# A hybrid retention/HGRN2 trunk on one core: where the HGRN2 state and row transfers are requested, and when the sample updates run

## The chip, the core and the metric

The kernel runs on one core of one Trainium2 chip. The metric is the device time of one execution in microseconds (us), taken as the median of several runs. One further execution was recorded by the hardware profiler; every row shown below comes from that execution, and its clock starts at the first instruction of the program.

## The reference, cut to what matters

One step of a decoder layer is computed for 272 prompt tokens (16 learned ones ahead of 256) and 8 sample tokens that go on from a stored state. Both groups use the same weights. The layer is a half-step feed-forward block, a mixer and a second half-step feed-forward block, each behind a residual and a layer norm.

```python
x <- LN1(alpha*x + 0.5*SwiGLU_1(x))
x <- LN2(alpha*x + Mixer(x))
x <- LN3(alpha*x + 0.5*SwiGLU_2(x))

# Mixer: x @ w_in, 2048 -> 10*2048, cut into
# [q_ret | k_ret | v_ret | g_ret | q_hg | f_hg | i_hg | g_hg | gate_ret | gate_hg]
def hgrn2_chunk(S, q, k, v, logf):
    b = jnp.cumsum(logf.astype(jnp.float32), axis=2)
    ...
    A = jnp.einsum('bhid,bhjd,bhijd->bhij', q, k, decay)
    o = jnp.einsum('bhij,bhjv->bhiv', A, v) + jnp.einsum('bhid,bhdv->bhiv', q * jnp.exp(b).astype(q.dtype), S)
    ...
    S_new = jnp.exp(b_last[:, :, 0, :, None]) * S + jnp.einsum('bhjd,bhjv->bhdv', k_dec, v)
```

The change lies in the HGRN2 half of the mixer. It has 16 heads with a 128x128 state each. For a sample token the chunk has one position, so its new state is `f * S + k v^T`, with `f` and `k` one number per state row and `v` one row of 128 numbers; its output is `q` times the new state. Eight samples make eight such states per head, 512 KB, which come from memory, are updated and go back.

## The kernel before, in words

**The weight stream.** Nearly all of the time is TensorE multiplying a stream of weight blocks of 128x128. `stream` fetches them eight at a time: a 512 KB transfer into a buffer `raw` (L185, issued on SyncE's queue), a cast to a rounded high part `whi` on ScalarE (L188) and the rest `wlo` on VectorE (L189). `dense` (L218) then makes three matmuls per block: high by high, high by low, low by high. `raw`, `whi` and `wlo` have three buffers each. A transfer into `raw` therefore waits for the `wlo` three fetches earlier, and a cast waits for TensorE to be done with the buffer three fetches earlier. Eight blocks are 24 matmuls.

**The mixer.** The projection with `w_in` runs over eight units `u`, each with two HGRN2 heads and one retention head. For each unit `project` runs the groups f, q_h, i_h, q_r, k_r, v_r, each two output tiles over 16 values of `k`, and then the gate groups of the unit before. In the trace the accumulators of these groups are named `pj_f`, `pj_q_h` and so on.

**Threads and steps.** The mixing itself is written as generators, `mix_hg(u, ...)` and `mix_ret(u, ...)`, that are interleaved with the projection. After each `k` of a group `dense` calls `pump`, which counts every thread down by one and resumes those that are due. `yield n` in a generator means: go on `n` steps later. A step of a two-tile group is six matmuls of the weight stream. TensorE runs in exactly the order in which the code issues its instructions. The order on the other engines, and on SyncE's queue of transfers, is made by a scheduler out of that same program; each engine and the queue then work strictly in order.

**The HGRN2 thread.** It scales q and k by levels, makes the score group and goes on as follows.

- The score group, `blocks` (L817 to L827) and `upper` (L843 to L853): 80 small products with an output `pl` in PSUM, issued without a weight matmul between them. Products in plain float32 take two matmul instructions each, and every matmul instruction has a weight load of its own.
- `fill` (L829, for head 0 and then head 1): VectorE moves part of `pl` into the score tile `acc` (`acch` in the trace), by masks, six instructions each plus one multiplication. `keep` (L857) moves the rest on ScalarE.
- `turned(h)` (L966): transposes of K and a ScalarE copy into `kts[h]` (`kth`).
- `gate()` (L975): the factors f and k of the sample tokens as columns of `meta`.
- `samples(h)` (L984): for each of eight samples, a scaling of the state `smh` on ScalarE (L988) and the addition of the outer product on VectorE (L989), which reads the rows `vbh`; then the store `out_sgs`.
- The prompt states `Ss` (`pst` in PSUM), the sample outputs `pq`, and the prompt outputs.

**The four transfers per unit.** `load(h)` (L765) asks for the states of head `h` (`smh`, 512 KB, L771) and `values(h)` (L773) for the eight rows of `v`, spread over all partitions (`vbh`, 512 KB, L776). `smh` shares its two buffers with two operands of the score group (`Qm`), `vbh` with another (`kept`).

**A tie.** `load(1)` and `values(1)` first let GpSimd copy one column of a result into the target buffer (L770 from `acc`, L775 from `kts`). The transfer writes over that column, so it can't be issued before the copy, and the copy can't run before the result is there. The queue is in order, so a transfer that waits for its tie also holds up what stands behind it.

Units 0 and 1 have other waiting times than the steady units 2 to 7 (`steady = u > 1`).

Of the kernel before, what the change touches and what calls it, by code (L numbers as in the profile page):

```python
# [18 lines left out]
P = 128  # L19
# [109 lines left out]
def trunk(ctx: ExitStack, tc: tile.TileContext, A, O):  # L129
    nc = tc.nc  # L130
# [12 lines left out]
    def mx_bank(name):  # L143
        return ps_m.tile([P, 512], F32, tag="mx", name=name)
# [59 lines left out]
    def dense(block, nk, outs, xhi, xlo, cols=slice(0, T), hook=None, parts_in_turn=False):  # L204
        n = len(outs)
        if isinstance(cols, slice):
            cols = [cols] * n
        for k in range(nk):
            todo = []
            for i in range(n):  # L210
                wh, wl = block()
                h, l = xhi[k][cols[i]], xlo[k][cols[i]]
                o = pairs(outs[i][:, : 2 * h.shape[1]])
                todo.append([(o, wh, h, k == 0, False), (o, wh, l, False, False), (o, wl, h, False, k == nk - 1)])

            for x in zip(*todo) if parts_in_turn else todo:
                for o, w, t, start, stop in x:
                    nc.tensor.matmul(o, w, t, start=start, stop=stop)  # L218
            if hook is not None:
                hook(k)  # L220
# [59 lines left out]
    class Norm:  # L280
# [96 lines left out]
        def first(self, block, outs, x0s):  # L377


            n = self.n  # L380

            def hook(k):
                if k == 5:
                    self.stats()

            dense(block, KC, outs, xh, xl, [slice(x0, n + 2) for x0 in x0s], hook)
            ys = self.corrected(outs, x0s)
            for c in range(KC):
                d = self.d[c]
                sub(d, d, self.mean)  # L390
                nc.vector.scalar_tensor_tensor(
                    out=d, in0=d, scalar=self.g[:, c : c + 1], in1=self.r, op0=ALU.mult, op1=ALU.mult)
            return ys

        def second(self, block, outs, x0s, into=()):
            dense(block, KC, outs, xh, xl, [slice(x0, self.n + 2) for x0 in x0s])
            self.normalise()
            return self.corrected(outs, x0s, into)
# [148 lines left out]
    with tc.tile_pool(name="yp", bufs=1) as yp:  # L547
# [7 lines left out]
        with tc.tile_pool(name="mp", bufs=1) as mp:  # L555
# [7 lines left out]
            def tmp(name, shape=(P, T), bufs=1, dt=F32, tag=None):  # L563
                if name in rows:
                    rows[name] = rows[name][1:] + rows[name][:1]
                    return rp.tile(list(shape), dt, tag=rows[name][-1], name=name)
                return mp.tile(list(shape), dt, tag=tag or name, name=name, bufs=bufs)
# [80 lines left out]
            def evacuate(n, c0, c1, o0, o1, b0, b1):  # L648
# [14 lines left out]
                elif n == "i_h":  # L663
                    v = st.pop("i_h", None)
                    if v is None:
                        v = tmp("v", (P, 2, T))
                        nc.scalar.copy(v[:, 0, :], o0)
                        nc.scalar.copy(v[:, 1, :], o1)

                    start(mix_hg(c0 // 2, st["f"], st["k"], st["q"], v), {0: 20, 2: 46}.get(c0, 4))  # L670
                elif n in ("q_r", "k_r"):
                    sc, w, x0 = (1.0, TL, NMETA) if n == "q_r" else (KSC, T, 0)
# [73 lines left out]
            def mix_hg(u, f, k, q, v):  # L746
# [15 lines left out]
                acc = tmp("acch", (P, 2 * SEQ))  # L762
                sms, vbs = [], []

                def load(h):  # L765

                    sms.append(tmp("smh", (P, NS, P), bufs=2))
                    vbs.append(tmp("vbh", (P, NS, P), bufs=2))
                    if h:
                        nc.gpsimd.tensor_copy(sms[h][:, 0, :1], acc[:, 31:32])  # L770
                    nc.sync.dma_start(sms[h], A["sg"][2 * u + h])  # L771

                def values(h):  # L773
                    if h:
                        nc.gpsimd.tensor_copy(vbs[h][:, 0, :1], kts[h][:, 0, :1])  # L775
                    nc.sync.dma_start(vbs[h], vrow[h].partition_broadcast(P))  # L776


# [21 lines left out]
                def join(s):  # L800
                    _, m, t2 = sides(s)
                    Ts[2 * s] = tmp(f"T{2 * s}", (P, 2, m))
                    mul(Ts[2 * s], t2[:, :, :, 0], t2[:, :, :, 1])
# [25 lines left out]
                def fill(half, s, h):  # L829
                    a = acc[:, 2 * P * h : 2 * P * (h + 1)]  # L830
                    if s == 1:
                        nc.vector.tensor_tensor(
                            out=a.rearrange("p (b j c) -> p b j c", b=2, j=4),
                            in0=half[:, :, 48:].unsqueeze(2).to_broadcast([P, 2, 4, 32]),
                            in1=ident.rearrange("p (j c) -> p j c", j=4).unsqueeze(1).to_broadcast([P, 2, 4, 32]), op=ALU.mult)
                    for i, (sl, mi) in enumerate(((s, MASKS[s][0]), (2 * s, MASKS[2 * s][0]), (2 * s, MASKS[2 * s][1]))):
                        n = 16 // sl
                        nc.vector.copy_predicated(
                            a.rearrange("p (b j n t s) -> p b j n t s", b=2, j=4, t=2, s=sl)[:, :, :, :, 1, :],
                            msk[:, mi, :P].rearrange("p (b j n s) -> p b j n s", b=2, j=4, s=sl),  # L840
                            half[:, :, 16 * i : 16 * i + 16].rearrange("p b (n s) -> p b n s", s=sl).unsqueeze(2).to_broadcast([P, 2, 4, n, sl]))
# [104 lines left out]
                scale_k(64)  # L946
                scale_q(64)
                join(64)
                load(0)
                values(0)  # L950
                for h in range(2):
                    if u:
                        fill(first(h), 1, h)
                    fill(second(h), 4, h)
                    yield 4
                    if h == 0:
                        load(1)
                for s in (16, 32, 64):
                    keep(tops[s], s)
                yield 15 if u == 1 else 2  # L960
# [3 lines left out]
                kts = []  # L964

                def turned(h):  # L966
                    kt = tmp("kth", (P, 2, P), bufs=2)
                    kts.append(kt)
                    pt = mx_bank("ptk")
                    for b in range(2):  # L970
                        t0 = NMETA + b * P
                        nc.tensor.transpose(pt[:, b * P : (b + 1) * P], K[:, h, t0 : t0 + P], ident)
                    nc.scalar.copy(kt, pt[:, : 2 * P].rearrange("p (b f) -> p b f", b=2))

                def gate():  # L975
                    pt = mx_bank("ptm")
                    x = pt[:64, :P]
                    nc.tensor.transpose(x, meta.rearrange("p h t -> p (h t)"), ident)
                    for i in range(2):
                        nc.gpsimd.tensor_copy(meta[:, :, NMETA + NS * i : NMETA + NS * (i + 1)], fk[:, i])  # L980
                    for i in range(2):
                        upper_upper_lower(km[:, i, :], x[32 * i : 32 * i + NMETA], 32 * i)

                def samples(h):  # L984
                    vb, sm = vbs[h], sms[h]
                    for b in range(NS):
                        at = NMETA + b
                        nc.scalar.activation(sm[:, b, :], sm[:, b, :], AF.Copy, scale=meta[:, h, at : at + 1])  # L988
                        nc.vector.scalar_tensor_tensor(  # L989
                            out=sm[:, b, :], in0=vb[:, b, :], scalar=meta[:, h, at + NS : at + NS + 1], in1=sm[:, b, :],  # L990
                            op0=ALU.mult, op1=ALU.add)
                    nc.sync.dma_start(O["sgs"][2 * u + h], sm)

                turned(0)
                yield 2
                turned(1)
                values(1)
                yield (11, 10, 5)[min(u, 2)]
                gate()
                samples(0)  # L1000
                yield (6, 6, 4)[min(u, 2)]
                samples(1)
                yield (4, 5, 6)[min(u, 2)]

                Ss = []
                for h in range(2):
# [9 lines left out]
                            out=S[:, b + 1, :], in0=S[:, b, :], scalar=Tt[:, h, b : b + 1],  # L1016
                            in1=pst[:, (b + 1) * P : (b + 2) * P], op0=ALU.mult, op1=ALU.add)
                    nc.sync.dma_start(O["sgp"][2 * u + h], S[:, 2, :])
                yield (8, 6, 52)[min(u, 2)]
                pq = mx_bank("pq")  # L1020
                for h in range(2):
                    for b in range(NS):
# [339 lines left out]
```

## Time and profile before

| what | value |
|---|---|
| median of three runs | 2591.33 us (2587.07 to 2593.44) |
| the profiled execution, its own time | 2588.29 us |
| its span, first to last instruction | 2586.5 us |
| TensorE busy | 2560.9 us, 99% |
| VectorE, ScalarE, GpSimd busy | 66%, 54%, 2% |
| transfers on SyncE's queue, share of 16 DMA engines | 63.3% |
| projection with `w_in`, eight units | about 770 to 1787 us |

The chain of waits is followed back from the last instruction; "issue" in it is time in which an engine waited for nothing that the profile names. In the timeline a row is one instruction, or several of one kind merged (xN); the number in square brackets is the idle time ahead of it and what ended it. A window's row gives for each engine the busy time and the number of instructions, then the granted TensorE clock, the share of the DMA engines' time and the rate in GB/s.

### The profile page before, as it was taken

The page shows a single profiled execution, that of the slowest core. Times are in us where ns is not written, and L with a number is a line of the kernel's source. Part 1 is how long each engine was busy: PE and PEld are TensorE (multiplying, and loading weights), DVE is VectorE, ACT ScalarE, POOL GpSimd, SP SyncE. Part 2 cuts the span into 40 slices and gives each one's busy share as a digit, 9 for nine tenths or more (in the row PEclk, how much of TensorE's full clock was granted, in tenths as well). Part 3 has the DMA queues.
Part 4 walks back from the last instruction along what each step waited for, and adds up shares of the span by engine and source line. Part 5 has one row for each costly group of instructions (what it writes and reads, how often), then busy time and mean ns, then how long its engine had stood idle before and what let it go on. Part 6 is the DMA issues. An engine that isn't in the chain of part 4 may idle for free.

```text
span 2586.5 us, 56251 instructions
## 1 busy us (share of the span) xinstructions
PE 2560.9 (99%) x23424; PEld 2541.4 (98%) x23424; DVE 1701.5 (66%) x2827; ACT 1392.2 (54%) x2186; POOL 50.4 (2%) x136
## 2 busy tenths in 40 slices
PE   9999999999999999999999999999999999999999
PEld 9999999999999999999999999999999999999998
DVE  6544445475579878777777777777985555556555
ACT  5444444444456767766666666665564444444444
POOL 0000000000000000000000000000000000000000
PEclk9999999999999999999999999999999999999999
DMA  7555555555566776767676767676566666656664
GB/s 242 186 182 187 185 183 187 182 186 182 185 199 196 273 272 224 252 204 255 202 259 212 259 199 262 211 240 196 191 190 198 194 195 196 196 195 195 196 196 148
DMA packets 156896, 536.26 MB, mean 207 GB/s; under 512 B 17952, under 2 KB 25952, under 8 KB 156640
## 3 DMA queue, kind: packets, MB, share of 16 engines
q1 hardware_dynamic: 156352, 532.37, 63.3%
q8 instruction: 183, 3.00, 0.5%
q14 instruction: 73, 0.60, 0.1%
q10 hardware_dynamic: 288, 0.29, 0.0%
HBM read 501.99 MB, written 30.61 MB: 206 GB/s over the span
## 4 chain that ended last, share of the span: by engine, by line
PE 93%; DVE 4%; issue 1%; DMA 1%; ACT 1%; POOL 0%; SPq 0%; ACTq 0%; DVEq 0%
PE up L218 36%; PE dn L218 18%; PE pj_q_r L218 3%; PE pj_g_r L218 3%; PE pj_a_r L218 3%; PE pj_k_r L218 3%; PE wo L218 3%; PE pj_g_h L218 3%; PE pj_a_h L218 3%; PE pj_v_r L218 3%; PE pj_i_h L218 3%; PE pj_q_h L218 3%; PE pj_f L218 3%; DVE wlo L189 1%; DVE xl L421 0%
## 5 line engine op out<-in xcount | busy, mean ns | idle before, releaser
L189 DVE TENSOR_TENSOR wlo<-raw,whi 128x1024 fp32r<-128x1024 f32 (+1 forms) x869 | 1063.2, 1224 | 763.6 <-ACT whi L188 760.5
L188 ACT CAST whi<-raw 128x1024 fp32r<-128x1024 f32 (+1 forms) x870 | 905.4, 1042 | 924.0 <-PE up L218 410.9
L218 PE MATMUL up<-xh,wlo 128*128 128x280 f32 (+1 forms) x2624 | 725.8, 280 | 0.4 <-DVE wlo L189 0.3
L218 PE MATMUL up<-xh,whi 128*128 128x280 f32 (+1 forms) x2624 | 726.2, 280 | 0.0
L218 PE MATMUL up<-xl,whi 128*128 128x280 f32 (+1 forms) x2624 | 725.5, 279 | 0.0
L218 PEld LDWEIGHTS up<-xh,wlo 128*128 128x128 f32 x2624 | 492.6, 189 | 1.0 <-DVE wlo L189 1.0
L218 PEld LDWEIGHTS up<-xh,whi 128*128 128x128 f32 x2624 | 493.0, 189 | 0.1
L218 PEld LDWEIGHTS up<-xl,whi 128*128 128x128 f32 x2624 | 492.8, 189 | 0.0
L218 PE MATMUL dn<-hh,whi 128*128 128x280 f32 (+1 forms) x1376 | 384.7, 280 | 0.0
L218 PE MATMUL dn<-hl,whi 128*128 128x280 f32 (+1 forms) x1376 | 384.3, 279 | 0.0
L218 PE MATMUL dn<-hh,wlo 128*128 128x280 f32 (+1 forms) x1376 | 384.3, 279 | 0.0
L218 PEld LDWEIGHTS dn<-hh,whi 128*128 128x128 f32 x1376 | 260.1, 189 | 0.1
L218 PEld LDWEIGHTS dn<-hl,whi 128*128 128x128 f32 x1376 | 260.1, 189 | 0.1
L218 PEld LDWEIGHTS dn<-hh,wlo 128*128 128x128 f32 x1376 | 260.1, 189 | 0.0
L218 PE MATMUL pj_k_r<-xh,whi 128*128 128x280 f32 x256 | 75.1, 293 | 0.0
L218 PE MATMUL pj_g_r<-xh,whi 128*128 128x264 f32 x256 | 74.0, 289 | 0.0
L218 PE MATMUL pj_k_r<-xl,whi 128*128 128x280 f32 x256 | 73.3, 286 | 0.0
L218 PE MATMUL pj_v_r<-xh,whi 128*128 128x280 f32 x256 | 73.3, 286 | 0.0
L218 PE MATMUL pj_k_r<-xh,wlo 128*128 128x280 f32 x256 | 73.2, 286 | 0.0
L218 PE MATMUL pj_v_r<-xh,wlo 128*128 128x280 f32 x256 | 72.4, 283 | 0.3 <-DVE wlo L189 0.3
L218 PE MATMUL pj_g_h<-xh,whi 128*128 128x264 f32 x256 | 72.7, 284 | 0.0
L218 PE MATMUL pj_v_r<-xl,whi 128*128 128x280 f32 x256 | 72.3, 283 | 0.0
(419 smaller groups left out, 5276.9 us busy)
## 6 DMA issues: line engine op xcount, KB each, us to landing
raw<-in_w_up SPq DMA_DIRECT2D x343, 512.0 KB, 3.5
raw<-in_w_in SPq DMA_DIRECT2D x320, 512.0 KB, 4.2
raw<-in_w_dn SPq DMA_DIRECT2D x172, 512.0 KB, 3.4
smr<-in_sr SPq DMA_DIRECT2D x32, 512.0 KB, 5.1
out_srs<-smr SPq DMA_DIRECT2D x32, 512.0 KB, 6.9
raw<-in_w_out SPq DMA_DIRECT2D x32, 512.0 KB, 3.6
vbr<-vrd SPq DMA_DIRECT2D x32, 256.0 KB, 4.1
smh<-in_sg SPq DMA_DIRECT2D x16, 512.0 KB, 5.7
```

Of the source, the lines that this page charges most:

```text
L188: nc.scalar.copy(hi[:, j:jn, :], raw[:, j:jn, :])
L189: nc.vector.tensor_tensor(out=lo[:, j0:j1, :], in0=raw[:, j0:j1, :], in1=hi[:, j0:j1, :].bitcast(F32), op=ALU.subtract)
L218: nc.tensor.matmul(o, w, t, start=start, stop=stop)
```

## The change

Three things are changed, all in `mix_hg`.

1. All four transfers of a unit are now tied, and all stand behind the score group. The states of head 0 are requested behind the first `fill` and tied to `acc` of head 0. The rows of head 0 are requested behind the second `fill` and tied to `acc` of head 1. The states of head 1 are requested with `turned(0)` and tied to `kts[0]`. The rows of head 1 keep their place behind `turned(1)` and their tie to `kts[1]`.
2. In the steady units `turned(1)` comes 2 steps later and the sample updates 6 steps later than before (2 + 5 becomes 4 + 9). In units 0 and 1 the sum stays as it was (2 + 11 and 2 + 10 against 4 + 9, one step more in unit 1).
3. The prompt states come 5 steps later in the steady units, and the wait ahead of `pq` is shortened by 5, so that `pq` stands where it stood.

```diff
                     vbs.append(tmp("vbh", (P, NS, P), bufs=2))
-                    if h:
-                        nc.gpsimd.tensor_copy(sms[h][:, 0, :1], acc[:, 31:32])
+                    nc.gpsimd.tensor_copy(sms[h][:, 0, :1], kts[0][:, 0, :1] if h else acc[:, 31:32])
                     nc.sync.dma_start(sms[h], A["sg"][2 * u + h])
 
                 def values(h):
-                    if h:
-                        nc.gpsimd.tensor_copy(vbs[h][:, 0, :1], kts[h][:, 0, :1])
+                    nc.gpsimd.tensor_copy(vbs[h][:, 0, :1], kts[1][:, 0, :1] if h else acc[:, 2 * P + 31 : 2 * P + 32])
                     nc.sync.dma_start(vbs[h], vrow[h].partition_broadcast(P))
...
                 join(64)
-                load(0)
-                values(0)
-                for h in range(2):
+                for h, ask in enumerate((load, values)):
                     if u:
                         fill(first(h), 1, h)
                     fill(second(h), 4, h)
+                    ask(0)
                     yield 4
-                    if h == 0:
-                        load(1)
                 for s in (16, 32, 64):
                     keep(tops[s], s)
                 yield 15 if u == 1 else 2
...
                 turned(0)
-                yield 2
+                load(1)
+                yield 4
                 turned(1)
                 values(1)
-                yield (11, 10, 5)[min(u, 2)]
+                yield 9
                 gate()
                 samples(0)
                 yield (6, 6, 4)[min(u, 2)]
                 samples(1)
-                yield (4, 5, 6)[min(u, 2)]
+                yield (4, 5, 5)[min(u, 2)]
...
-                yield (8, 6, 52)[min(u, 2)]
+                yield (8, 6, 47)[min(u, 2)]
                 pq = mx_bank("pq")
```

What this makes of the transfers on SyncE's queue is the same in all steady units. Before, this stood there in unit 2 from the first row store on (`raw` with a number is a fetch of eight weight blocks, `vh0d` and `vh1d` the rows of `v` on their way through memory; TensorE comes to the score group of the unit at about the time at which `raw_12753` is issued):

```order
L730 DMA vh0d<-vsm 8x128
L185 DMA raw_12723<-in_w_in 128x1024
L730 DMA vh1d<-vsm 8x128
L776 DMA vbh<-vh0d 128x1024
L185 DMA raw_12753<-in_w_in 128x1024
L771 DMA smh<-in_sg 128x1024
L185 DMA raw_12821<-in_w_in 128x1024
L771 DMA smh<-in_sg 128x1024
L185 DMA raw_12868<-in_w_in 128x1024
L185 DMA raw_12916<-in_w_in 128x1024
L776 DMA vbh<-vh1d 128x1024
L185 DMA raw_12946<-in_w_in 128x1024
```

The same place of the queue now:

```order
L185 DMA raw_12759<-in_w_in 128x1024
L185 DMA raw_12800<-in_w_in 128x1024
L770 DMA smh<-in_sg 128x1024
L185 DMA raw_12857<-in_w_in 128x1024
L774 DMA vbh<-vh0d 128x1024
L185 DMA raw_12904<-in_w_in 128x1024
L770 DMA smh<-in_sg 128x1024
L185 DMA raw_12952<-in_w_in 128x1024
L774 DMA vbh<-vh1d 128x1024
L185 DMA raw_12987<-in_w_in 128x1024
```

`raw_12759` now is the fetch that was `raw_12753`. The rows of head 0 (`vbh<-vh0d`) moved back by three weight fetches, the states of head 0 by one, those of head 1 by two and the rows of head 1 by one; exactly one of the four stands between two fetches.

On ScalarE the sample updates stood here in unit 2 before, between the casts of the weights (`kth` is `kts`, `km` comes from `gate`, `v<-pj_v_r` is the first copy that the retention thread needs):

```order
L973 COPY kth<-ptk 128x256
L188 CAST whi_12869<-raw_12868 128x8x128
L723 CAST km<-ptm 16x128
L724 CAST km<-ptm 16x128
L988 ACTIVATE smh<-smh,meta 128x128 x5
L723 CAST km<-ptm 16x128
L724 CAST km<-ptm 16x128
L988 ACTIVATE smh<-smh,meta 128x128
L188 CAST whi_12917<-raw_12916 128x8x128
L988 ACTIVATE smh<-smh,meta 128x128 x7
L188 CAST whi_12947<-raw_12946 128x8x128
L988 ACTIVATE smh<-smh,meta 128x128 x3
```

And now, up to that copy:

```order
L723 CAST km<-ptm 16x128
L724 CAST km<-ptm 16x128
L983 ACTIVATE smh<-smh,meta 128x128 x2
L188 CAST whi_12953<-raw_12952 128x8x128
L723 CAST km<-ptm 16x128
L724 CAST km<-ptm 16x128
L983 ACTIVATE smh<-smh,meta 128x128 x6
L188 CAST whi_12988<-raw_12987 128x8x128
L983 ACTIVATE smh<-smh,meta 128x128 x7
L188 CAST whi_13054<-raw_13053 128x8x128
L983 ACTIVATE smh<-smh,meta 128x128
L1009 COPY Sh<-pst 128x128 x2
```

The sixteen scalings are the same sixteen; they now end two casts later, behind that of `raw_13053`. Before, the last of them stood behind the cast of `raw_12946`, with two more casts between them and the first `v` copy of the retention thread (L684); now that copy is the next row.

TensorE has the same matmuls; the transposes of `turned` and `gate` and the products `pst` stand 2, 6 and 5 steps later among the weight matmuls, and two waiting instructions are added in its program. GpSimd has sixteen more one-column copies in all.

## The prediction

> **What bounds the kernel now.** I read the page first, then TensorE's waits, then the chain of waits in order of time, and last the stretches that it pointed to. The page says that TensorE is the bound, and it gives the queue on which the program's own instructions are fetched (packets, MB, share of the DMA engines' time):
>
> ```profile
> span 2586.5 us, 56251 instructions
> PE 2560.9 (99%) x23424; PEld 2541.4 (98%) x23424; DVE 1701.5 (66%) x2827; ACT 1392.2 (54%) x2186; POOL 50.4 (2%) x136
> q8 instruction: 183, 3.00, 0.5%
> ```
>
> What TensorE waited for (us in total, times, longest) is one thing; every other cause of its waits adds up to 1.0 us or less:
>
> ```profile
> PE pj_q_r L218 <- issue: 15.1, 6, 3.1
> ```
>
> The chain shows where these six lie: each time a few matmuls behind the score group `pl` of a steady unit, in `pj_q_r` (start, length, what):
>
> ```profile
> 1003.27 1.12 PE pl L827 x89
> 1006.12 1.85 issue
> ...
> 1100.56 10.80 PE pj_q_h L218 x96
> ...
> 1131.45 1.07 PE pl L827 x89
> 1133.26 1.21 PE pj_q_r L218 x9
> 1134.47 3.13 issue
> ...
> 1263.85 1.07 PE pl L827 x89
> ...
> 1267.10 2.67 issue
> ...
> 1394.62 1.07 PE pl L827 x89
> ...
> 1398.10 2.32 issue
> ...
> 1523.23 1.07 PE pl L827 x89
> ...
> 1526.93 2.99 issue
> ...
> 1653.89 1.07 PE pl L827 x86
> ...
> 1657.81 2.18 issue
> ```
>
> The six sum to 15.14 us. There is more behind them. From one `pl` to the next it takes 128.18, 132.40, 130.77, 128.61 and 130.66 us; less the gap in each, 126.3, 129.3, 128.1, 126.3 and 127.7. So a unit without a gap is 126.3 us, and the gaps of 3.13, 2.67 and 2.99 are followed by a further loss of 3.0, 1.8 and 1.4 us. The windows show what it is (the third-last column is the granted clock, then the DMA share, then GB/s):
>
> ```profile
> 1003.27:1007.96 4.69, 2.85 (x167) 2.56 (x167) 4.14 (x8) 1.43 (x2) 0.00 (x0) 1.00 0.77 290
> 1131.45:1137.60 6.15, 3.02 (x170) 2.73 (x170) 5.07 (x16) 1.01 (x1) 0.00 (x0) 0.94 0.84 280
> 1137.60:1143.50 5.90, 5.90 (x26) 5.90 (x27) 1.52 (x4) 1.04 (x1) 0.19 (x1) 0.50 0.44 151
> 1394.62:1400.42 5.80, 3.48 (x175) 3.19 (x174) 4.72 (x14) 1.02 (x1) 0.00 (x0) 1.00 0.95 331
> 1523.23:1529.92 6.69, 3.70 (x175) 3.41 (x176) 5.30 (x16) 1.01 (x1) 0.19 (x1) 0.96 0.92 300
> ```
>
> After the gap of 3.13 us the clock is 0.50, and 26 matmuls take 5.9 us instead of 2.9 (the `pj_q_h` row gives 10.80/96 = 0.1125 us for one). After 2.32 us it stayed at full. The whole loss is 15.14 + 6.2 = 21.3 us; that is all the change can win here.
>
> **What I take the gap to be.** The q8 row has 183 packets; TensorE has 2 x 23424 instructions, so a packet brings 256.0 of them. The weight stream uses up 256 instructions (128 matmuls with their loads) in 128 x 0.1125 = 14.4 us. From `pl` at 1131.45 to the `pj_q_r` row at 1133.26, 1.8 us, pass the 160 matmuls of the score group (170 in the window's row, less 10 of the stream), 320 instructions. A border between two packets that falls early into the group thus needs the next packet within 2 to 3 us. The transfers just behind 1131.3 and just behind 1134.0, by queue:
>
> ```profile
> q1 hardware_dynamic: 186, 0.68, 80.1%
> ```
> ```profile
> q1 hardware_dynamic: 157, 0.57, 77.1%
> q8 instruction: 1, 0.02, 6.0%
> ```
>
> The first is 1131.3 to 1134.0, without a packet on q8; the second is 1134.0 to 1136.3, with one; TensorE stopped at 1134.47 and went on at 1137.60. So the instructions came late, at a time when the data queue kept the DMA engines 77 to 95% busy (the windows above). What stood on the queue:
>
> ```profile
> 1127.80 0.34 SPq L185 DMA_DIRECT2D raw<-in_w_in  x1
> 1128.18 0.32 SPq L730 DMA_DIRECT2D vh1d<-vsm  x1
> 1129.90 0.33 SPq L776 DMA_DIRECT2D vbh<-vh0d  x1
> 1131.05 0.33 SPq L185 DMA_DIRECT2D raw<-in_w_in  x1
> 1132.85 0.33 SPq L771 DMA_DIRECT2D smh<-in_sg  x1
> 1133.75 0.33 SPq L185 DMA_DIRECT2D raw<-in_w_in  x1
> 1137.96 0.33 SPq L771 DMA_DIRECT2D smh<-in_sg  x1
> ```
>
> **The change, part by part.** *The rows and states of head 0 leave the place ahead of the fetch.* `vbh` was requested 1.5 us ahead of the score group and is now three weight fetches later; `smh` was requested 1.4 us into the group and now waits for the first `fill`. The weight fetches of 1131.05 and 1133.75 stay, since they wait for buffers. The trace doesn't show the fetch without those two transfers, so I bound it. The busiest stretch of the projection gives the price of 512 KB:
>
> ```profile
> 840.00:845.00 5.00, 5.00 (x99) 4.78 (x98) 3.67 (x9) 4.99 (x6) 0.00 (x0) 1.00 1.01 404
> ```
>
> At 404 GB/s, 524 288 bytes keep all engines for 1.30 us. From below: nothing is saved, if the two weight fetches alone delay the packet as much. From above: both transfers were ahead of it, 2.60 us. I take 1.30 us per gap: `vbh` was ahead of the fetch in every unit, while `smh` was issued 1.1 us before 1134.0 and has moved little by then. The program also has two waiting instructions more on TensorE, both ahead of unit 2's score group; they shift the packet's border by one matmul against the group and take 0.11 us from the time allowed. The gaps become 0.66, 1.94, 1.48, 1.13, 1.80 and 0.99 us, together 8.0. All are below the 2.32 us that left the clock at full, so the 6.2 us go as well. Gain: 21.3 - 8.0 = 13.3 us. At the bounds: both saved leaves 0, 0.64, 0.18, 0, 0.50 and 0, so 20.0; none saved costs 0.7.
>
> [...]
>
> *Ties on the queue.* Four transfers per unit now wait for a GpSimd copy, and one weight fetch stands behind each. What such waits cost the queue before, beside what the weight fetches wait for anyway:
>
> ```profile
> SPq L185 <- DVE wlo L189: 1278.7, 580, 3.8
> ...
> SPq L771 <- POOL smh L770: 22.8, 6, 3.9
> ...
> SPq L776 <- POOL vbh L775: 13.3, 6, 2.7
> ```
>
> The weight fetches waited for a free buffer 580 times; two ties per unit held the queue for up to 3.9 us, and TensorE's waits show no weight that came late for it in the steady units. The new ties end before the buffer of the next weight fetch is free: head 0's two are results that stand ahead of the next `wlo` or just behind it on VectorE. I cost them at nothing; the cover is the three buffers, and a tie held longer than the 3.9 us seen is a price without a row. GpSimd's sixteen copies fall into its 98% of idle time.
>
> *Sample updates 6 steps later.* A step is six matmuls, 0.675 us, so 4.05 us. The same 16 scalings on ScalarE and 16 additions on VectorE run; what counts is whether they are done before the retention thread's `v` copy:
>
> ```profile
> 1164.11 1.05 ACT L188 CAST whi<-raw 128x1024 fp32r<-128x1024 f32 x1 [1.77 <-PE pj_v_r L218]
> 1166.73 0.39 ACT L684 COPY v<-pj_v_r 128x280 f32<-128x280 f32 x1 [1.57 <-PE pj_v_r L218]
> ...
> 1194.91 1.05 ACT L188 CAST whi<-raw 128x1024 fp32r<-128x1024 f32 x1 [2.26 <-DMA raw<-in_w_in]
> ```
>
> ScalarE stood idle for 1.77 + 1.57 = 3.34 us there, waiting for TensorE, and takes most of the 4.05; the remaining 0.7 us fall on weight buffers that are full. Cost: nothing, at most 0.7 us in six units.
>
> *Units 0 and 1.* Their sample updates stay, but head 0's rows move from an early request into the saturated stretches (404 GB/s above). At most 1.30 us each; I take nothing, since head 0's states leave the same stretches a little later too.
>
> *The sum.* 2588.29 (the profiled execution's own time) - 13.3 = 2575.0 us. That execution is 3.0 us below the median of the three runs; the mean of all four times is 2590.0, and 2590.0 - 13.3 = 2577 is what I forecast.
>
> **The rivals.** *The gaps close.* Both transfers were ahead of the fetch: gain 20.0, 2570 us. For it: the DMA share is 0.92 and 0.95 in the windows of 1523 and 1394. Against it: two weight fetches remain.
>
> *The gaps stay,* because the weight fetches alone delay the packet, or because something else makes them: 2590.0 + 0.7 = 2590.7 us. For it: in unit 2 the share was only 0.77 and there was a gap all the same. Against it: the gaps differ from 1.85 to 3.13 us at one and the same place of the program, so something outside TensorE sets their length.
>
> *The sample updates come too late,* the case that ends slower. Around 1194.91 ScalarE waits for weights that come just in time, so lateness that lasts until there would stop TensorE. If none of the idle time were usable, 4.05 us in six units are 24.3 us, against 13.3 won: 2601 us. It decides from 13.3/6 = 2.2 us of lateness per unit. Against it stands the 3.34 us of idle time ahead of the `v` copy.
>
> **How the numbers follow.** Forecast 0.50 (2573 to 2582); gaps close 0.18; gaps stay 0.20; samples late or weights held up 0.12. Forecast and closing are faster by more than 0.3% (7.8 us, about what a measurement can tell), 0.68; staying is within it, 0.20; lateness is slower, 0.12. The range goes from 2567, the closed gaps with 3 us of scatter between runs, to 2592, the gaps that stay; lateness is left out.
>
> **What the profile after would show.** Right: the "issue" waits of `pj_q_r` at the same place, six or fewer, about 8 us in total and none above 2.3; the clock full behind them; a unit 126 to 128 us from `pl` to `pl`. Wrong: "issue" still near 15 us, or new waits of TensorE for `wlo`, in `pj_v_r` or in the gate groups, which would mean late samples or held-up weights.

## The result and the profile after

The changed kernel takes 2576.74 us (median of 6 runs, 2575.6 to 2580.53) against 2587.7 us of the kernel before beside it (median of 6, 2582.48 to 2593.44): a ratio of 0.9958, 95% interval 0.9943 to 0.9972. It is faster by 11.0 us, or 0.42%. The forecast was 2577.

The page of the kernel after; its own time was 2577.58 us, against 2588.29 before:

```profile
span 2575.8 us, 56267 instructions
PE 2557.2 (99%) x23424; PEld 2536.8 (98%) x23424; DVE 1703.7 (66%) x2827; ACT 1391.9 (54%) x2186; POOL 52.7 (2%) x152
q8 instruction: 183, 3.00, 0.5%
```

The same 183 instruction packets and the same 23424 matmuls; only GpSimd has 16 instructions more, the new ties. What TensorE waited for (us in total, times, longest):

```profile
PE pj_q_r L218 <- issue: 7.8, 6, 1.7
...
PE po L1032 <- DVE Sh L1011: 0.6, 1, 0.6
...
PE pl L851 <- DVE Q L240: 0.3, 1, 0.3
```

The six gaps are still there, but half as long (15.1 before). The two other rows are new and small. The gaps stand at the same place as before, a few matmuls behind the score group (chain of waits, start, length, what):

```profile
1003.53 1.12 PE pl L825 x90
...
1006.78 0.52 issue
...
1130.89 1.07 PE pl L825 x89
...
1132.71 1.10 PE pj_q_r L218 x8
1133.81 1.70 issue
1135.51 3.62 PE pj_q_r L218 x16
...
1260.81 1.07 PE pl L825 x85
...
1263.94 1.62 issue
...
1388.87 1.07 PE pl L825 x89
...
1392.23 1.69 issue
...
1516.84 1.07 PE pl L825 x88
...
1520.43 1.25 issue
...
1644.37 1.07 PE pl L825 x89
...
1648.18 1.03 issue
```

The stretches from `pl` to `pl`, and the 3.42 us at half clock behind unit 3's gap of 1.70 us (length, busy time of PE, PEld, DVE, ACT and POOL, then granted clock, DMA share, GB/s):

```profile
1003.53:1130.89 127.36, 126.53 (x1278) 124.75 (x1282) 100.93 (x198) 86.65 (x162) 6.38 (x14) 1.00 0.71 240
1130.89:1260.81 129.92, 128.22 (x1280) 126.37 (x1283) 98.77 (x194) 84.75 (x158) 5.27 (x14) 0.99 0.70 232
1260.81:1388.87 128.06, 126.44 (x1279) 124.69 (x1283) 98.56 (x194) 84.87 (x158) 5.26 (x14) 1.00 0.71 236
1388.87:1516.84 127.97, 126.28 (x1280) 124.62 (x1283) 98.65 (x194) 84.73 (x158) 5.27 (x14) 1.00 0.70 236
1516.84:1644.37 127.53, 126.28 (x1279) 124.62 (x1283) 98.67 (x194) 84.59 (x158) 5.46 (x16) 1.00 0.70 237
...
1135.82:1139.24 3.42, 3.42 (x18) 3.42 (x17) 1.47 (x7) 0.24 (x1) 0.19 (x1) 0.50 0.30 65
```

TensorE's busy time is 126.3 to 126.5 us in four of the five stretches and 128.2 in unit 3: there 3.42 us ran at half clock behind a gap of only 1.70 us.

Where the time came from, by the two profiled executions (their spans differ by 10.7 us): up to unit 2 the kernel after is 0.26 us later (1003.53 against 1003.27). From unit 2's `pl` to unit 7's it takes 640.84 us in place of 650.62, a gain of 9.78. From there to the end 1.18 us are won, unit 7's gap being 1.15 us shorter (2.18 to 1.03). Of the 9.78 us, the five gaps give 6.18 (12.96 to 6.78) and the busy time of TensorE, which is nearly all the half clock, 3.91 (the five stretches of before had 126.33, 129.27, 128.10, 126.29 and 127.67); other small waits take 0.31 back.

The transfers by queue just ahead of and just behind 1133.1 us, in unit 3 of the kernel after:

```profile
q1 hardware_dynamic: 41, 0.14, 87.8%
```
```profile
q1 hardware_dynamic: 17, 0.06, 46.9%
q8 instruction: 1, 0.02, 21.4%
```

The first is 1132.7 to 1133.1, without a packet on q8; the second is 1133.1 to 1133.4, with one. TensorE went on at 1135.51. Before, the packet came after 1134.0, and it went on at 1137.60. On SyncE's queue only weight fetches are still requested close to the group; the four tied transfers follow behind them, with one fetch between each two (left out here):

```profile
1130.49 3.03 SPq L185 DMA_DIRECT2D raw<-in_w_in  x2
1137.43 0.33 SPq L770 DMA_DIRECT2D smh<-in_sg  x1
...
1141.78 0.36 SPq L774 DMA_DIRECT2D vbh<-vh0d  x1
...
1145.38 0.42 SPq L770 DMA_DIRECT2D smh<-in_sg  x1
...
1147.86 0.42 SPq L774 DMA_DIRECT2D vbh<-vh1d  x1
```

**The gap, counted.** Counted over TensorE's instructions in the trace (matmuls, weight loads and a few that only wait), the six gaps end at numbers 17857, 20417, 22977, 25537, 28097 and 30657. They are 2560 apart, ten packets of 256 exactly, while the score groups of neighbouring steady units begin 2556 or 2557 instructions apart. So the gap belongs to the border between two packets and not to a line of the program, and one border earlier lies inside the group: before, 79 to 98 instructions into its 320, after, 77 to 96. That earlier border is passed 0.4 to 0.5 us into the group. From there until TensorE goes on again took 4.4, 5.8, 5.6, 5.4, 6.3 and 5.7 us in units 2 to 7 before, and 3.5, 4.3, 4.4, 4.7, 4.5 and 4.5 us after. The difference is 1.2 us on the mean.

The trace also has the start of each instruction packet. It began 2.1, 2.3, 3.1, 3.2, 3.9 and 3.3 us behind that border before, and 1.1, 1.9, 2.2, 2.3, 2.3 and 2.2 us after. In all twelve cases TensorE went on 1.2 to 1.5 us after the end of the packet, so the length of the gap is the lateness of the packet. (The packet took 0.9 to 1.0 us, but 2.2 us in unit 3 before, which is part of that gap of 3.13 us.) In the whole program before, no packet begins more than 34 of TensorE's instructions ahead of its border, so here the instructions come one packet ahead and not several. In units 3 to 7 after, a weight fetch was requested 0.7 to 0.8 us ahead of the border; in unit 2, with the shortest gap of 0.52 us, the nearest one was requested 2.3 us ahead.

### The profile page after: what moved, and what is told of

Its sections match the earlier page's. It is cut to its first block, busy times and chain, and to the rows that moved or that the text cites. A ratio compares the mean times of both kernels' runs of the same rounds, so it can differ in the third digit from the quotient of the medians.

```text
span 2575.8 us, 56267 instructions
## 1 busy us (share of the span) xinstructions
PE 2557.2 (99%) x23424; PEld 2536.8 (98%) x23424; DVE 1703.7 (66%) x2827; ACT 1391.9 (54%) x2186; POOL 52.7 (2%) x152
## 4 chain that ended last, share of the span: by engine, by line
PE 93%; DVE 4%; ACT 1%; issue 1%; DMA 1%; POOL 0%; ACTq 0%; DVEq 0%
PE up L218 36%; PE dn L218 19%; PE pj_q_r L218 3%; PE wo L218 3%; PE pj_g_r L218 3%; PE pj_a_r L218 3%; PE pj_g_h L218 3%; PE pj_a_h L218 3%; PE pj_k_r L218 3%; PE pj_i_h L218 3%; PE pj_v_r L218 3%; PE pj_f L218 3%; PE pj_q_h L218 3%; DVE wlo L189 1%; ACT whi L188 1%
```

## The experiments

The theory after the result: the packet that is asked for at the border inside the group comes late behind data transfers; the rows of head 0, 512 KB queued just ahead of the group, delayed it by another 1.2 us; what is left comes from the weight fetches. The rivals: the backlog is without effect and something else in the change won the time; the gap belongs to the place in the program and not to the border; the later sample updates are part of the gain or of a hidden cost.

| kernel | median us (runs) | ratio to before, 95% | gaps behind or in `pl`, us |
|---|---|---|---|
| after | 2576.74 (6) | 0.9958 (0.9943 to 0.9972) | 7.8 |
| after, rows of head 0 early | 2587.18 (10) | 0.9990 (0.9980 to 1.0001) | 14.0 |
| after, states of head 0 early | 2580.68 (4) | 0.9954 (0.9938 to 0.9969) | 8.0 |
| before, border moved | 2571.58 (4) | 0.9924 (0.9910 to 0.9938) | none |
| after, border moved | 2571.26 (5) | 0.9922 (0.9910 to 0.9935) | none |
| before, border moved, cheaper | 2568.99 (6) | 0.9923 (0.9910 to 0.9936) | none |
| after, border moved, cheaper | 2569.09 (6) | 0.9924 (0.9911 to 0.9937) | none |
| after, sample updates at old steps | 2576.76 (6) | 0.9956 (0.9942 to 0.9970) | 8.4 |
| after, border moved the wrong way | 2592.03 (10) | 1.0009 (0.9999 to 1.0019) | 13.9 |
| before, rows of head 0 late | 2577.26 (5) | 0.9961 (0.9947 to 0.9974) | 7.6 |

The kernel before had 2587.7, 2591.0, 2590.2 and 2588.6 us as its medians beside the four groups of runs, so medians of different groups are comparable to some 3 us, and the ratios say more.

### One transfer moved back: the rows of head 0

```diff
-                for h, ask in enumerate((load, values)):
+                values(0)
+                for h in range(2):
...
-                    ask(0)
+                    if h == 0:
+                        load(0)
```

and `values(0)` without its tie.

> The kernel after, but the rows of head 0 are requested without a tie ahead of the fills, where they stood before the change; states, samples and the other ties stay as after. Theory (the instruction packet waits behind data transfers that are queued ahead of it): 512 KB more ahead of the packet, 1.30 us per gap, so the issue waits of pj_q_r go from 7.8 to about 15 us, part of the half clock returns, and the time goes from 2577 to 2585 to 2589 us. Rival (the queue's backlog is without effect, the gain came from something else in the change): issue waits 7 to 9 us, time 2575 to 2579.

TensorE's first wait:

```profile
PE pj_q_r L218 <- issue: 14.0, 6, 3.1
```

The gaps came back, 6.2 us of them or 1.03 us per gap, and with them all or nearly all of the gain: the ratio's interval reaches 1. The rival that the backlog is without effect falls.

### One transfer moved back: the states of head 0

```diff
-                for h, ask in enumerate((load, values)):
+                load(0)
+                for h in range(2):
...
-                    ask(0)
+                    if h:
+                        values(0)
```

and `load(0)` without its tie.

> The kernel after, but the states of head 0 are requested without a tie ahead of the fills as before the change, and the rows of head 0 then behind the second fill. Theory: the request is issued only about 1 us ahead of the fetch, so between nothing and 1.30 us per gap, issue waits 8 to 12 us, time 2577 to 2584 us, less than with the rows early. Rival (backlog without effect): issue waits 7 to 9 us, time 2575 to 2579. Rival (any request in that place costs the same): issue waits about 15 us, time as with the rows early.

```profile
PE pj_q_r L218 <- issue: 8.0, 6, 1.8
```

Nothing moved: 8.0 against 7.8 us, and a ratio of 0.9954 against 0.9958. It is the low end of what the theory gave; by itself it would also fit the rival that the run before ruled out. In unit 3 this request went out 1.1 us behind the border. A request of the same size, issued a little later, didn't delay the packet: what seems to have counted in these two runs (14.0 and 8.0 us of gaps) is whether it stood ahead of the packet, not the traffic as such.

### No transfer moved, the border moved

```diff
                     pt = mx_bank("ptk")
+                    for _ in range({1: 22, 7: 10}.get(u, 0)):
+                        nc.tensor.matmul(pt[:32, 2 * P : 2 * P + 16], ident[:, :32], ident[:, :16], start=True, stop=True)
```

A plain float32 product takes two matmul instructions with a load each here (in the trace before, the score group's 80 products are 160 matmuls, and there are 23424 matmuls and as many loads), so the 44 in unit 1 make 176 instructions, and the 20 in unit 7 the 80 that are left to 256. Nothing else differs from the kernel before.

> The kernel before, with no transfer moved; 44 matmuls of 32x16 without use stand in unit 1's turned and 20 in unit 7's, so that units 2 to 7 find the border of the 256-instruction packets 157 to 178 instructions into the score group of 320 in place of 79 to 98, and all that follows unit 7 is where it was. Theory (the gap is a late instruction packet): the packet then has the time of the 100 instructions ahead of the group, about 5 us or more, to arrive; the issue waits behind pl go from 15.1 to 0 to 2 us, the half clock goes, 2588 becomes 2567 to 2571 us (1.4 us of it for the useless matmuls, 128 loads and matmuls at 11 ns). Rival (the gap belongs to the place in the program, the border is without meaning): issue waits about 15 us, time 2588 to 2591.

The largest wait of TensorE, now at the start of the program; the chain around unit 4's group; and two stretches from `pl` to `pl`:

```profile
PE pw L515 <- DVE eps_h L163: 1.0, 1, 1.0
```
```profile
1258.46 1.07 PE pl L827 x89
1259.52 0.75 PE pl L853 x52
1260.27 2.90 PE pj_q_r L218 x24
1263.17 4.29 PE pj_k_r L218 x36
```
```profile
1132.44:1258.46 126.02, 126.02 (x1280) 124.56 (x1283) 98.52 (x194) 84.56 (x158) 6.57 (x12) 1.00 0.74 239
1258.46:1384.47 126.01, 126.01 (x1279) 124.54 (x1282) 98.51 (x194) 84.54 (x158) 6.55 (x12) 1.00 0.73 240
```

No gap in any unit, the clock at full, and a unit of 126.02 us in which TensorE never stands, with all four transfers where the kernel before has them and the DMA share even higher. So the gap is a packet border that falls unluckily, and the rival that it belongs to the place in the program falls. The time, 2571.58, is 0.6 us above the expected stretch, because the useless matmuls cost more than reckoned:

```profile
949.01 1.50 PE ptk L971 x44
```

That is 34 ns for each load with its matmul, where 11 had been taken from the score group.

This run, which moved only the border, is 16 us or more faster than the kernel before (the lower end of the interval).

### The border moved and the transfers moved

The same useless matmuls, in the kernel after.

> The kernel after with the same useless matmuls; the border then lies 157 to 178 instructions into the group of units 2 to 7. Theory: issue waits from 7.8 to 0 to 1 us, no half clock, time 2567 to 2571 us, about the same as the kernel before with the useless matmuls, since the moved transfers have nothing left to save. Rival (border without meaning): 2577 to 2580 us. Rival (the moved transfers save something beside the gaps): clearly below the kernel before with the useless matmuls.

It took 2571.26 us in the same group of runs: with the gaps closed the moved transfers save nothing. All that the change wins, it wins by shortening these six gaps, with the half clock behind them.

### The same with cheaper matmuls, on both

```diff
-                    for _ in range({1: 22, 7: 10}.get(u, 0)):
+                    for i in range({1: 22, 7: 10}.get(u, 0)):
-                        nc.tensor.matmul(pt[:32, 2 * P : 2 * P + 16], ident[:, :32], ident[:, :16], start=True, stop=True)
+                        j = 32 * (i % 4)
+                        nc.tensor.matmul(
+                            pt[j : j + 32, 2 * P : 2 * P + 16], ident[:, :32], ident[:, :16],
+                            start=True, stop=True, tile_position=(0, j))
```

> The kernel before with the same 64 useless matmuls as in the earlier pair, but each on the next of the four 32-column places, as the score group's own matmuls are. In the earlier pair 88 loads and matmuls took 3.0 us and 40 about 1.4 us, 34 ns each; the score group needs 11 ns each. Theory (they cost only their own time, the gaps stay closed): 2571.6 less 2.9 us, 2567 to 2570 us, no issue waits behind pl. Rival (the place of the extra work hides it, or something else holds these kernels at 2571): 2570 to 2573.

> The kernel after with the cheaper useless matmuls. Theory (the moved transfers save nothing but the gaps): the same as the kernel before with them within 2 us, 2567 to 2570. Rival (the moves cost or save something of their own): a difference of 2 us or more between the two.

In the chain of the first of them:

```profile
949.95 0.50 PE ptk L972 x41
```

12 ns each in place of 34. The medians are 2568.99 and 2569.09 us, 2.6 and 2.2 less than with the dearer matmuls. The ratios to the kernel before don't resolve that step, but the row of the trace does. These two are the fastest kernels here, about 7.7 us below the kernel after, and they don't differ: the change is not needed for it.

### The sample updates at their old steps

```diff
-                yield 4
+                yield 2
                 turned(1)
                 values(1)
-                yield 9
+                yield (11, 10, 5)[min(u, 2)]
...
-                yield (4, 5, 5)[min(u, 2)]
+                yield (4, 5, 6)[min(u, 2)]
...
-                yield (8, 6, 47)[min(u, 2)]
+                yield (8, 6, 52)[min(u, 2)]
```

> The kernel after, but the sample updates and what follows them stand at their old steps; the four requests stay where the change put them. Theory (the sample updates' six steps cost and save nothing): 2575 to 2579 us, issue waits 7 to 9 us. Rival (the later sample updates are part of the gain): 2580 us or more. Rival (they cost, hidden in the gain): 2574 or less.

```profile
PE pj_q_r L218 <- issue: 8.4, 6, 2.0
```

2576.76 against 2576.74 us: the six steps cost and save nothing that can be measured. The wait of `po` for `Sh` of 0.6 us is gone in this kernel. It is gone as well in two kernels that keep the moved steps (rows of head 0 early; after, border moved), so where it came from is open.

### The border moved the wrong way

```diff
                     pt = mx_bank("ptk")
+                    for i in range({1: (6, 5), 7: (27, 26)}.get(u, (0, 0))[h]):
+                        j = 32 * (i % 4)
+                        nc.tensor.matmul(
+                            pt[j : j + 32, 2 * P : 2 * P + 16], ident[:, :32], ident[:, :16],
+                            start=True, stop=True, tile_position=(0, j))
```

> The kernel after with 11 useless matmuls in unit 1 (44 instructions) and 53 in unit 7, in place of 44 and 20: the packet border lies 33 to 52 instructions into the group of units 2 to 7, so that the next border lies inside the group too, 256 instructions or 1.4 us on. In the kernel after, border to border took 2.1 to 3.0 us without the gap, and with the gap 4.1 us in units 3 to 7 (2.6 in unit 2). Theory (the packet comes a fixed time after the border, whatever TensorE does meanwhile): gaps of 4.1 - 1.4 = 2.7 us in five units and 1.2 in unit 2, issue waits 13 to 16 us, now inside pl; with some half clock 2585 to 2591 us, as slow as the kernel before though no transfer moved back. Rival (the gap's size comes from the transfers alone): issue waits about 8 us, 2577 to 2580.

```profile
PE pl L851 <- issue: 12.3, 5, 3.5
PE pj_i_h L218 <- DVE wlo L189: 2.0, 2, 1.5
PE pj_g_h L218 <- DVE wlo L189: 1.6, 3, 0.8
PE pl L851 <- DVE wlo L189: 1.6, 1, 1.6
```

Two borders now lie inside the group, and the gap is inside it as well. Together the six are 13.9 us (unit 2's is put down to `wlo`, at the same instruction of the packet), within the 13 to 16 expected, and the kernel is as slow as the one before, with every transfer where the change put it. But the packet did not come a fixed time after the border: the single gaps run from 1.4 to 3.5 us where 2.7 was expected, and 1.2 in unit 2. (The expectation also took the time from border to border after as 2.6 and 4.1 us; the trace has 3.5 and 4.3 to 4.7.) The packets' starts differ as well. They lie 0.8, 0.7, 0.7, 2.7, 2.1 and 2.3 us behind the border. The nearest weight fetch ahead of the border was requested 0.50 and 0.51 us before it in units 3 and 4, and 0.54, 0.56 and 0.59 us before it in units 5 to 7; in unit 2 there was none within 2 us. Units 4 and 5, the request and the gap:

```profile
1265.33 0.33 SPq L185 DMA_DIRECT2D raw<-in_w_in  x1
1393.15 3.03 SPq L185 DMA_DIRECT2D raw<-in_w_in  x2
```
```profile
1267.41 1.52 issue
1395.25 3.48 issue
```

A fetch requested a few hundredths of a microsecond earlier against the border thus goes with a packet 1.5 to 2.1 us later, as if the packet took its turn behind what was requested ahead of it. This is read off five units of one trace; no run was made for it.

Not all of the time is in the gaps, either. This profiled span is 12.2 us longer than that of the kernel after: 4.1 up to unit 2's group, 4.8 from there to unit 7's, and 3.3 behind it. The part up to unit 2 holds only a quarter of a microsecond of added matmuls (22 loads and matmuls at 12 ns). Weights that came late, as the rows of `pj_i_h` and `pj_g_h` show, are in the rest. Why they came late is open; `pj_i_h` waited 1.2 us or more in six other kernels here as well (0.5 in the kernels before and after), so it need not be this edit.

### One transfer of the change alone

```diff
                 load(0)
-                values(0)
                 for h in range(2):
...
                     fill(second(h), 4, h)
+                    if h:
+                        values(0)
                     yield 4
```

with the tie of the kernel after, in the kernel before.

> The kernel before with one transfer moved: the rows of head 0 are requested behind the second fill, tied to its result, as in the kernel after; the states of both heads, the rows of head 1 and the sample updates stay as before. Theory (the rows of head 0 alone stand ahead of the late instruction packet): issue waits 7 to 10 us, time 2575 to 2581 us, the whole gain of the change or all but 3 us of it. Rival (the states of head 0 count as well when head 1's states follow them as early as before): issue waits 11 us or more, time 2582 us or more.

```profile
PE pj_q_r L218 <- issue: 7.6, 6, 1.6
```
```profile
1132.47:1260.38 127.91, 126.31 (x1279) 124.65 (x1283) 98.33 (x194) 84.82 (x158) 5.70 (x13) 1.00 0.71 236
```

A ratio of 0.9961 against 0.9958 of the whole change: this one line is the change. The half clock is away in unit 3 as well here, behind a gap of 1.60 us.

## Why the prediction was right, and where not

- **What bounds the kernel:** right. The gaps and the half clock behind them made up the whole difference of the two traces, and the kernel without gaps has 126.02 us per unit where 126.3 was read off as stall-free.
- **What the gap is:** right, and shown from two sides. Moving the border closed the gaps (15.1 us to none) or lengthened them (7.8 to 13.9) without a transfer being moved; moving one transfer halved them (15.1 to 7.6) without the border being moved.
- **The price of 1.30 us per gap, for the rows and not the states:** right in kind and close in size. Forecast 0.66, 1.94, 1.48, 1.13, 1.80 and 0.99, in sum 8.0; measured 0.52, 1.70, 1.62, 1.69, 1.25 and 1.03, in sum 7.8. One price for all gaps was too simple: single ones are off by up to 0.56 us, and these errors cancel in the sum. Moving the rows back alone cost 1.03 us per gap, moving the states back cost none, and moving the rows alone brought the gain. Between the bounds set then, none and both transfers, the choice by the order on the queue held.
- **The half clock entirely gone:** the step that was mis-sized. The 6.2 us were to go because every gap would be below 2.32, a gap that had left the clock at full. Unit 3 kept about 1.9 us of it (128.22 less 126.3) behind a gap of 1.70, and TensorE's busy time fell by 3.9 us over units 2 to 6. The remaining 2.3 us are what the gain fell short by, 11.0 us by the medians against 13.3. The length of a gap alone did not decide whether the clock halved: behind 1.70 us it did, behind 2.32 us it did not. The two also differ in where they lie (below): the gap of 2.32 us lay in two windows of the clock's grid, with 1.56 and 0.76 us, that of 1.70 us in one.
- **The ties at nothing:** right. No wait for weights appeared in the steady units, and the kernel with one tie more than before (rows of head 0) takes the same as the one with all of them.
- **The sample updates six steps later at nothing:** right; 2576.76 with the old steps.
- **Units 0 and 1 at nothing:** 0.26 us later at unit 2. The wait of `po` for `Sh`, 0.6 us, was not foreseen; one of 0.8 us (`pvr` for `rlo`) went away.
- **The rivals:** that the gaps close falls, since weight fetches alone leave 7.8 us. That they stay falls with the measured 7.8 against 15.1. That the sample updates come too late falls with their run.
- **The number** came out 0.3 us from the measured median, with two deviations that nearly cancel: the gain was 2.3 us too large, and the base, the mean of the four times then known (2590.0), was 2.3 us above the median of the kernel before in the new runs (2587.7). That it came so close is luck; the mechanism is not.

## What to carry to other kernels

In this kernel a dense group of tiny instructions (320 in 1.8 us) held a packet border 77 to 98 instructions in, and TensorE ran into the next border before the packet was there. Look for "issue" gaps that repeat at one place, count the instructions between them, and if they are a multiple of 256, as the 2560 here, try to move the border before moving any data. Here 176 cheap instructions ahead of the first such group, and 80 behind the last, won 20 us; rearranging the transfers, the costlier edit, won 11. If the border can't be moved, try first the transfers requested last ahead of the border: here 512 KB ahead of it added 1.03 us per gap, and 512 KB requested behind it none.

## What the runs showed of the hardware

**The time of a packet.** From the border to the instructions of the late packet took 3.5 to 4.7 us with weight fetches alone ahead and 4.4 to 6.3 with 512 KB more. The weight stream, with 14.4 us per packet, hid that: in the kernels before and after all "issue" waits of TensorE's matmuls are the six behind the score groups (15.1 and 7.8 us). The 320 instructions in 1.8 us didn't.

**As much data, requested a little later, cost nothing.** In unit 3 of the two kernels that moved one transfer back, the rows were requested 1.9 us ahead of the group (1131.21 against 1133.15) and the states 1.4 us into it (1136.86 against 1135.46), about 1.1 us behind the border. 512 KB each; the first added 1.03 us per gap, the second none. The two transfers also differ in kind (rows spread over all partitions, states read as they lie), which no run separates; that the place decided is a reading that rests also on the weight fetches in the kernel with the border moved the wrong way (0.50 and 0.51 us ahead of the border with packets 0.7 us behind it, 0.54 to 0.59 us with packets 2.1 to 2.7 us behind it). No run shows why the packet came later with more ahead of it.

**The clock after a gap.** In the kernel before, the granted clock fell to half at 1136.83, 1269.95 and 1529.37 us, for 6.83, 3.41 and 3.41 us. These times lie 39 and 76 times 3.413 us apart, and in the kernel after the half clock began and ended on such a grid too, at another offset (1135.82 and 1139.24 us, and again at the end of the program from 2572.83 us, 420 steps on). So in these traces the clock changed on a grid of 3.41 us; a window below is the stretch from one point of it to the next, and the gaps are compared by how much of each falls into one window. The gap of 1.70 us in the kernel after lay whole in one (the first row below; the window behind it is the row at half clock in the section on the result). With the rows of head 0 early, unit 6 had a gap of 3.11 us, which lay in two windows with 1.91 and 1.20 us (the grid taken from that trace's half clock, which began at 1266.9 us, 75 steps earlier), and the clock stayed at full:

```profile
1132.41:1135.82 3.41, 1.71 (x31) 1.42 (x21) 3.38 (x10) 0.00 (x0) 0.00 (x0) 1.00 0.69 232
```
```profile
1524.41 3.11 issue
```
```profile
1522.90:1526.32 3.42, 1.51 (x14) 1.31 (x12) 3.39 (x13) 0.00 (x0) 0.00 (x0) 1.00 0.85 302
1526.32:1529.73 3.41, 2.21 (x19) 2.21 (x20) 0.88 (x5) 0.85 (x1) 0.19 (x1) 1.00 0.44 120
```

The six kernels with gaps behind `pl` have 36 such gaps in their traces, and the clock halved at seven of them. With 2.00 us or more of a gap in one window it halved every time (five times), below 1.70 us never. In between it halved at 1.70 and 1.79 us and stayed at full at 1.91 and 1.94 us, so the idle time in a window does not tell the two apart, and what does is open. In the first row above TensorE was busy for 1.71 of the 3.41 us, and half clock followed all the same. With the border moved the wrong way, TensorE had from 1393.55 to 1399.14 us nothing but 2.11 us of the score group's small matmuls and a gap of 3.48 us between them, and the clock stayed at full (1.00 from 1393.55 to 1523.44 us).
